# A hybrid mLSTM and delta-rule block: each engine's instruction order made with the framework's timeline model

## The chip, the cores and the metric

The kernel runs on one core of one Trainium2 chip. A core has a matrix engine (TensorE, PE in the profile; its weight loads are listed as PEld), three engines for elementwise work (VectorE or DVE, ScalarE or ACT, GpSimd or POOL) and a sync engine (SP) that here only issues transfers. Each engine works through a list of its own; engines wait for each other and for transfers through semaphores. The metric is device time in microseconds for one execution of the program, lower is better; the time of a kernel is the median of its runs.

## What is computed

One encoder layer over 256 tokens of width 2048, batch 1, in float32, followed by a final RMSNorm. Cut to what matters:

```python
mod = silu(c) @ ada_w + ada_b                       # 2048 -> 6 x 2048
h = rms_norm(x, norm_mix_w) * (1 + scale_m) + shift_m
proj = h @ w_in                                     # 2048 -> about 18500 columns
h_a = bidirectional(mlstm_chunkwise, ...)           # 4 heads, keys of 256, values of 512
y_a = (sigmoid(a_o) * rms_norm(h_a)) @ w_branch_a
qkv = silu(centred_depthwise_conv(b_qkv, gdn_conv_w))
o_b = bidirectional(gated_delta_chunkwise, ...)     # 16 heads of 128
y_b = (rms_norm(o_b) * silu(b_z)) @ w_branch_b
x = x + gate_m * ((g_a * y_a + g_b * y_b) @ w_out)
hf = rms_norm(x, norm_ffn_w) * (1 + scale_f) + shift_f
x = x + gate_f * ((silu(gt) * up) @ w_down)         # gt, up = split(hf @ w_gate_up), 5632 wide
return rms_norm(x, norm_final_w)
```

## The kernel before

**Weights and matmuls.** Every large weight is read once from HBM, in pieces of 1 MB, on SP's queue into one of three buffers called `raw`. For the projections the kernel splits both operands into a high and a low half: ACT copies a piece into a rounded high half `wh` (lines 155 and 180), DVE subtracts it from the piece and gives the low half `wl` (lines 156 and 181), and PE adds three products: high by high, low activation by high weight, high activation by low weight (lines 159 and 161 in `fjob`, lines 198, 199 and 201 in `tjob`). There are three buffers of `wh` and three of `wl`, each for half a piece. `fjob` has the weights as stationary operand and gives features by tokens, 256 columns wide; `tjob` has the activations as stationary operand and gives tokens by features, 512 columns wide, with two accumulators for the two halves of the tokens. Accumulators live in a pool of four PSUM banks (`acc`), the small work of the recurrences in another four (`g`).

**Stages.** The first stage computes the norm, the modulation of the mixer and the first 16 column blocks of the input projection in one loop over the 16 blocks of the width (`first`, line 509; loads `ra` and `raw`, DVE lines 470 and 474). Then come the gates, and the delta rule over the 16 heads in four groups: `gdn_phase1` per head, `gdn_invert` and `gdn_blocks` per group, `gdn_phase2` for each pair of heads (its PE steps are called `p`, `pa`, `pb`, `pc`, `po`, `px`). These are chains of small steps through PE, DVE, ACT and POOL. Between their steps the kernel traces pieces of the rest of the input projection, by counts written out by hand: Python generators (`fills`, `stream`) are advanced by `fill(n)` and `drive(gen, n)`. The same is done with mLSTM and the first branch projection (`y_b`). After that follow the second branch projection (`y_a`), the output projection (`o`, weights `wo`), the second norm (`normed`, `moved`, `low`), gate and up projection (`gt`, `up`), and the down projection (`d`), each group of 512 columns after another.

**Background.** The modulation vectors that are needed later are made on DVE (`ada_part`, line 124): 1 MB of `ada_w` is loaded by SP into a `raw` buffer and multiplied by the row of `silu(c)` with a sum along the way. `pump` and `sums` put such a product in after every second or fourth piece of a projection, or at points written out.

**What sets the order.** The Python code only traces instructions, in one sequence for all engines. When the `with tile.TileContext(...)` block of `kernel` is left, the framework makes from that sequence one list for each engine. It plays the program on a model of the machine: each time an engine of the model can take an instruction, it is given, of those whose inputs and buffers are there in the model, the one traced earliest. The list of an engine is the order in which it was given its instructions in that play, and buffers of a pool (`raw`, `wh`, `wl`, `acc`, `g`) go to whoever comes first in it. So the traced sequence is a priority, and the model's times decide where a later instruction goes ahead of an earlier one. Semaphores are put in afterwards, for the order that came out. On the chip each list is then fixed.

**Pins.** `order(ins)` calls `tc.keep_in_program_order`, which keeps an instruction behind everything traced before it on its engine, whatever the model says. Pinned are nearly all vector and scalar instructions and loads of the first stage, the steps of `gdn_invert` and `gdn_blocks`, the decays of mLSTM, the splits `o_split`, the residual of the last column group, the second norm, and the output. Where `tjob` is called with `early`, the first conversions are pinned as well. All other instructions, nearly all matmuls among them, are free.

## Time and profile before

| what | us |
|---|---|
| median of 3 runs | 2047.38 |
| lowest and highest run | 2047.14 and 2054.85 |
| profiled execution, whole | 2052.6 |
| profiled execution, span from first to last instruction | 2050.5 |
| DVE, busy | 1394.8 |
| ACT, busy | 1047.7 |
| HBM read and written | 467.07 MB and 16.82 MB |

The page of the profile gives, for each engine, the time in which it ran at least one instruction. A matmul's record is longer than its share of the stream of matmuls, since they are pipelined: records overlap. "Idle before" is the time between the records of one engine, and the view of the waits says which engine's instruction or which transfer ended it. A matmul appears with the tile that it writes and the tiles that it reads; the same source line can belong to many jobs, so groups are told apart by the tile's name (`acc_b` is the accumulator of a job `b`, `raw_o` the buffer of a weight piece of a job `o`; `acc_o` stands both for mLSTM's output gate and for the output projection).

### The profile page before, as it was taken

The page shows a single profiled execution, that of the slowest core. Times are in us where ns is not written, and L with a number is a line of the kernel's source. Part 1 is how long each engine was busy: PE and PEld are TensorE (multiplying, and loading weights), DVE is VectorE, ACT ScalarE, POOL GpSimd, SP SyncE. Part 2 cuts the span into 40 slices and gives each one's busy share as a digit, 9 for nine tenths or more (in the row PEclk, how much of TensorE's full clock was granted, in tenths as well). Part 3 has the DMA queues.
Part 4 walks back from the last instruction along what each step waited for, and adds up shares of the span by engine and source line. Part 5 has one row for each costly group of instructions (what it writes and reads, how often), then busy time and mean ns, then how long its engine had stood idle before and what let it go on. Part 6 is the DMA issues. An engine that isn't in the chain of part 4 may idle for free.

```text
span 2050.5 us, 27063 instructions
## 1 busy us (share of the span) xinstructions
PE 1963.4 (96%) x10374; PEld 1711.0 (83%) x10374; DVE 1394.8 (68%) x2059; ACT 1047.7 (51%) x1582; POOL 106.4 (5%) x205
## 2 busy tenths in 40 slices
PE   8999999999999899999999998899999999999998
PEld 6887879988989788889878887678888888888886
DVE  5788776777888588765667777766656665555554
ACT  3147548755774667556443443464444444444443
POOL 0002210110101011101100000000000000000000
PEclk9999999999999999999999999999999999999999
DMA  9986664556667565766986677756766766555553
GB/s 400 420 323 214 194 202 155 179 183 226 235 216 227 180 214 213 236 234 248 368 298 229 218 261 286 279 189 242 259 236 253 254 230 225 197 204 201 202 203 142
DMA packets 78962, 485.64 MB, mean 237 GB/s; under 512 B 10585, under 2 KB 15969, under 8 KB 24433
## 3 DMA queue, kind: packets, MB, share of 16 engines
q1 hardware_dynamic: 63360, 450.95, 60.6%
q0 software_dynamic: 8160, 17.88, 3.8%
q10 hardware_dynamic: 7314, 15.10, 1.9%
q8 instruction: 81, 1.33, 0.3%
q14 instruction: 47, 0.39, 0.1%
HBM read 467.07 MB, written 16.82 MB: 236 GB/s over the span
## 4 chain that ended last, share of the span: by engine, by line
PE 67%; DVE 13%; DMA 11%; ACT 6%; issue 3%; POOL 1%; ACTq 0%; SPq 0%; DVEq 0%; POOLq 0%
PE acc_b L159 4%; PE acc_up L199 4%; PE acc_up L201 4%; PE acc_up L198 4%; PE acc_d L199 4%; PE acc_d L201 4%; PE acc_d L198 4%; PE acc_gt L199 4%; PE acc_gt L201 3%; PE acc_gt L198 3%; DMA ra<-ada 3%; PE acc_b L161 2%; DMA ada<-ada 1%; PE acc_yb L199 1%; PE acc_yb L201 1%
## 5 line engine op out<-in xcount | busy, mean ns | idle before, releaser
L181 DVE TENSOR_TENSOR wl_d<-raw_d,wh_d 128x1024 fp32r<-128x1024 f32 x88 | 107.5, 1225 | 105.3 <-ACT wh_d L180 103.1
L181 DVE TENSOR_TENSOR wl_up<-raw_up,wh_up 128x1024 fp32r<-128x1024 f32 x88 | 107.6, 1225 | 100.0 <-ACT wh_up L180 100.0
L124 DVE SCALAR_TENSOR_TENSOR ada<-ada,crow 128x2048 f32<-128x2048 f32 x64 | 146.4, 2287 | 19.5 <-DMA ada<-ada 19.4
L180 ACT ACTIVATE wh_d<-raw_d 128x1024 fp32r<-128x1024 f32 x88 | 92.9, 1056 | 124.5 <-PE acc_d L199 114.3
L181 DVE TENSOR_TENSOR wl_gt<-raw_gt,wh_gt 128x1024 fp32r<-128x1024 f32 x88 | 107.7, 1224 | 70.1 <-ACT wh_gt L180 68.6
L180 ACT ACTIVATE wh_up<-raw_up 128x1024 fp32r<-128x1024 f32 x88 | 92.9, 1056 | 119.9 <-PE acc_up L199 71.6
L159 PE MATMUL acc_b<-hh,wh_b 128*128 128x256 f32 x576 | 141.4, 288 | 9.3 <-ACT wh_b L155 7.7
L180 ACT ACTIVATE wh_gt<-raw_gt 128x1024 fp32r<-128x1024 f32 x88 | 92.9, 1055 | 108.7 <-PE acc_gt L199 61.3
L159 PE MATMUL acc_b<-hl,wh_b 128*128 128x256 f32 x576 | 138.9, 284 | 0.0
L199 PE MATMUL acc_gt<-wh_gt,hfl 128*128 128x512 f32 x352 | 136.3, 387 | 0.1
L198 PE MATMUL acc_gt<-wh_gt,hfh 128*128 128x512 f32 x352 | 135.2, 384 | 0.0
L199 PE MATMUL acc_up<-wh_up,hfl 128*128 128x512 f32 x352 | 133.6, 379 | 0.0
L198 PE MATMUL acc_up<-wh_up,hfh 128*128 128x512 f32 x352 | 133.5, 379 | 0.0
L198 PE MATMUL acc_d<-wh_d,ffh 128*128 128x512 f32 x344 | 130.8, 380 | 0.0
L199 PE MATMUL acc_d<-wh_d,ffl 128*128 128x512 f32 x344 | 130.7, 380 | 0.0
L159 PEld LDWEIGHTS acc_b<-hh,wh_b 128*128 128x128 f32 x576 | 114.4, 199 | 10.1 <-ACT wh_b L155 8.4
L509 PE MATMUL first<-x,raw 128*128 128x256 f32 x512 | 114.5, 382 | 7.7 <-ACT x L502 7.7
L509 PEld LDWEIGHTS first<-x,raw 128*128 128x128 f32 x512 | 96.2, 190 | 26.0 <-ACT x L502 13.7
L159 PEld LDWEIGHTS acc_b<-hl,wh_b 128*128 128x128 f32 x576 | 114.4, 199 | 0.0
L180 ACT ACTIVATE wh_o<-raw_o 128x1024 fp32r<-128x1024 f32 x64 | 66.2, 1054 | 77.1 <-DMA raw_o<-wo 44.9
L298 DVE SCALAR_TENSOR_TENSOR cv<-pad,pk,cv 128x256 f32<-128x256 f32 x192 | 90.8, 481 | 19.2 <-ACT cv L296 17.1
L156 DVE TENSOR_TENSOR wl_b<-raw_b,wh_b 128x1024 fp32r<-128x1024 f32 x72 | 86.8, 1219 | 24.6 <-ACT wh_b L155 24.2
(369 smaller groups left out, 5031.5 us busy)
## 6 DMA issues: line engine op xcount, KB each, us to landing
ada<-ada SPq DMA_DIRECT2D x64, 1024.0 KB, 4.9
raw_gt<-wgu SPq DMA_DIRECT2D x44, 1024.0 KB, 5.0
raw_up<-wgu SPq DMA_DIRECT2D x44, 1024.0 KB, 5.0
raw_d<-wd SPq DMA_DIRECT2D x44, 1024.0 KB, 4.9
raw_b<-winb SPq DMA_DIRECT2D x36, 1024.0 KB, 5.1
ra<-ada SPq DMA_DIRECT2D x32, 1025.0 KB, 15.7
raw<-win SPq DMA_DIRECT2D x16, 1024.0 KB, 14.5
raw_z<-wint SPq DMA_DIRECT2D x16, 1024.0 KB, 5.1
```

The lines of the kernel that those rows point to most:

```text
L124: V.scalar_tensor_tensor(raw, raw, 1.0, row_c[:, :D], ALU.mult, ALU.mult, accum_out=mod[:, c0 + b : c0 + b + 1])
L156: V.tensor_tensor(wl, raw[:, k0 : k0 + 8], wh.bitcast(F32), ALU.subtract)
L159: PE.matmul(o, wh[:, k], both(x, k0 + k).rearrange("p a b -> p b a"), start=k0 + k + i == 0, stop=False)
L161: PE.matmul(o, wl[:, k], both(hh, k0 + k).rearrange("p a b -> p b a"), start=False, stop=k0 + k == KB - 1)
L180: order(S.activation(wh, raws[u][:, k0 : k0 + 2], AF.Copy), early)
L181: order(V.tensor_tensor(wl, raws[u][:, k0 : k0 + 2], wh.bitcast(F32), ALU.subtract), early)
L198: order(PE.matmul(ps[t], tok(xh, kk, t), turns(wh[:, k]), start=kk == 0, stop=False), early and steps > 1)
L199: PE.matmul(ps[t], tok(xl, kk, t), turns(wh[:, k]), start=False, stop=False)
L201: PE.matmul(ps[t], tok(xh, kk, t), turns(wl[:, k]), start=False, stop=kk == last)
L298: V.scalar_tensor_tensor(cv, pd[:, i : i + T], w[i], cv, ALU.mult, ALU.add)
L509: PE.matmul(first[o], raw[:, o], x[:, b], start=b == 0 and o % 2 == 0, stop=b == KB - 1 and o % 2 == 1)
```

## The change

One argument is given where the context is opened:

```diff
-    with tile.TileContext(nc) as tc:
+    with tile.TileContext(nc, schedule_with_timeline_sim=True) as tc:
         hybrid_block(tc, *args)
```

By default the play that makes the lists runs on the framework's plain simulator, where an engine carries out one instruction at a time for a cost from a table. [...] Nothing else differs: the traced sequence, the pins, the pools and their sizes, and the instructions themselves are those of before. What can differ is the place of each free instruction in its engine's list, which tile gets which buffer of its pool and when, and so the waits that the framework puts in.

## The prediction

> **What bounds the kernel now.** I read the page first, then the windows view cut at the borders of the stages, then the waits of each engine inside a stage.
>
> ```profile
> span 2050.5 us, 27063 instructions
> PE 1963.4 (96%) x10374; PEld 1711.0 (83%) x10374; DVE 1394.8 (68%) x2059; ACT 1047.7 (51%) x1582; POOL 106.4 (5%) x205
> PE 67%; DVE 13%; DMA 11%; ACT 6%; issue 3%; POOL 1%; ACTq 0%; SPq 0%; DVEq 0%; POOLq 0%
> ```
>
> TensorE is the bound by a wide margin: it is busy for 1963.4 of 2050.5 us, and two thirds of the chain that ended last are its instructions. What a new order can win is therefore at most the 87.1 us in which it has no record. Where those lie shows in the windows view (PE, PEld, DVE, ACT, POOL busy with counts, then granted clock, DMA share, GB/s). The stages, by the first and last matmul of each, are: first projection; gates, delta rule and the rest of the input projection; mLSTM with the two branch projections; output projection and second norm; gate/up; down projection.
>
> ```profile
> 0.00:138.00 138.00, 127.65 (x555) 104.31 (x555) 94.08 (x112) 31.59 (x60) 2.41 (x12) 1.00 0.97 399
> 138.00:963.00 825.00, 786.87 (x4948) 709.22 (x4947) 628.25 (x1219) 535.84 (x954) 89.29 (x169) 0.98 0.62 209
> 963.00:1224.00 261.00, 252.03 (x1202) 211.15 (x1201) 179.41 (x223) 115.29 (x148) 14.69 (x24) 0.97 0.74 272
> 1224.00:1357.00 133.00, 113.65 (x487) 92.29 (x486) 97.39 (x125) 59.59 (x91) 0.00 (x0) 0.95 0.70 258
> 1357.00:1808.00 451.00, 450.94 (x2122) 392.64 (x2120) 269.42 (x248) 202.50 (x217) 0.00 (x0) 1.00 0.66 236
> 1808.00:2050.00 242.00, 232.29 (x1071) 201.41 (x1069) 126.27 (x136) 102.91 (x115) 0.00 (x0) 0.99 0.55 191
> ```
>
> Idle time is window less PE busy: 10.4, 38.1, 9.0, 19.4, 0.1 and 9.7 us, 86.7 together. Gate/up has none: 2122 matmuls in 451 us, one every 0.2125 us, at clock 1.00. So only the middle three stages, 66.5 us, can be moved by an order. The first stage is at 0.97 of the DMA engines, and its loads, vector work and conversions are pinned one behind the other by `order`; only its matmuls are free. The end of the last stage is the output, pinned too.
>
> **The change, part by part.** It adds and removes no instruction of the kernel's own: no matmul, conversion or DMA. What it moves is the place of every unpinned instruction on PE, ACT, DVE, SP and POOL, since each list is made by a play of the program through another model. A faithful model can win what an order can win, a wrong one can lose far more than that. So I price by stage.
>
> *Gate/up and down (693 us).* ACT has a conversion ready to start and waits until PE lets a buffer go:
>
> ```profile
> ACT wh_d L180 <- PE acc_d L199: 114.3, 75, 2.0
> ```
>
> 75 waits for 88 conversions mean that supply is ahead of PE almost always. I cost the new order here at 0. The cover is that wait, 114.3/75 = 1.5 us for each conversion, and three buffers of 12 matmuls each, 36 x 0.2125 = 7.7 us. An instruction put ahead of a conversion that takes longer than this would show as idle PE. Below nothing is excluded: there is no idle time to win.
>
> *Gates, delta rule and projections (825 us).* This is where the lists are least pinned. All waits of PE in this stage (us in total, times, longest):
>
> ```profile
> PE acc_b L159 <- ACT wh_b L155: 7.7, 4, 4.0
> PE acc_z L198 <- ACT wh_z L180: 4.8, 3, 2.8
> PE p L687 <- DVE R L659: 4.8, 2, 2.5
> PE vps L553 <- ACT vf L299: 3.5, 5, 1.7
> PE acc_o L201 <- DVE wl_o L181: 3.4, 1, 3.4
> PE acc_mb L201 <- DVE wl_mb L181: 2.4, 3, 1.2
> PE acc_z L201 <- DVE wl_z L181: 1.8, 2, 1.2
> PE acc_v L201 <- DVE wl_v L181: 1.7, 1, 1.7
> PE acc_b L161 <- DVE wl_b L156: 1.6, 1, 1.6
> PE acc_b L159 <- ACT ev_ma L311: 1.6, 1, 1.6
> PE p L696 <- DVE pt L688: 1.5, 1, 1.5
> PE px L770 <- ACT obt L772: 1.0, 1, 1.0
> PE pb L745 <- DVE r L746: 0.8, 1, 0.8
> PE acc_ma L201 <- DVE wl_ma L181: 0.8, 1, 0.8
> PE p L721 <- DVE pt L710: 0.3, 1, 0.3
> ```
>
> Two of the waits of ACT in the same stage:
>
> ```profile
> ACT wh_b L155 <- DMA raw_b<-winb: 15.0, 7, 6.0
> ...
> ACT wh_z L180 <- DMA raw_z<-wint: 11.3, 3, 6.3
> ```
>
> PE's rows sum to 37.7 us in 28 waits, 1.35 us each. Three kinds. (i) The waits for `wh_b` and `wh_z`, 12.5 us: the conversion itself waits for a landing, as these two rows show, so another order on ACT alone gains nothing. (ii) Those for the low halves `wl` (11.7) and `ev_ma` (1.6), 13.3 us: DVE or ACT was at something else, and an order can cure it. (iii) Those of the delta rule's chain (`p`, `vps`, `px`, `pb`), 11.9 us: PE stood at a step of the chain; an order that has a projection matmul in that place cures it if one was ready. The gain lies between 0 and 13.3 + 11.9 = 25.2 us. I take half, 12.6 us, as nothing in the trace shows that more was ready at those moments.
>
> Against it stand the waits that the new order makes itself. The trace of before cannot show them, and the bounds are wide: 0 if every instruction lands where it is wanted, and for one displaced instruction the longest wait above, 4.0 us. The nearest row is the mean, 1.35 us. DVE and ACT are 76% and 65% busy here (628.25 and 535.84 of 825), so a list drawn from another model misplaces something too; I take about as many as vanish, 9 x 1.35 = 12.2 us. What is queued behind such an instruction on DVE is the next `wl`, and behind that SP, since a `raw` buffer comes free only when its `wl` is made:
>
> ```profile
> SPq L177 <- DVE wl_z L181: 78.8, 10, 15.6
> ```
>
> A late `wl` thus delays a load as well, and the load the next conversion. Net for the stage: -12.6 + 12.2 = -0.4 us, with 25.2 us as the end on the gain's side; the other end is the rival on DVE below.
>
> Idle time is not all that a wait costs: clock 0.98 over 825 us is 16.5 us of full-clock work not granted, beside 38.1 us of idle, so each us of new idle may cost up to 1.43 us. I put this in the range, not in the sum. [...]
>
> *mLSTM and branch projections (261 us).*
>
> ```profile
> PE pxa L978 <- DVE hal L983: 3.6, 1, 3.6
> PE psc L922 <- DMA mkq<-kq_d: 3.5, 1, 3.5
> ```
>
> Two waits make 7.1 of the 9.0 us idle. The second is a landing; the first is a step with nothing else ready. Bounds: 7.1 us gained; lost, as much again. I take 0.
>
> *Output projection and second norm (133 us).*
>
> ```profile
> PE acc_o L198 <- ACT wh_o L180: 8.2, 5, 3.5
> PE pxn L1169 <- ACT xn L1162: 7.9, 7, 3.4
> PE acc_o L201 <- DVE wl_o L181: 3.2, 3, 1.8
> ```
>
> ```profile
> ACT wh_o L180 <- DMA raw_o<-wo: 44.9, 10, 8.5
> ```
>
> The norm (7.9) is pinned. The 11.4 us at `acc_o` have a landing behind them: ACT waits 44.9 us for `raw_o`, since loads of `wo` and of `ada` share the three `raw` buffers and the SP list. If the new SP list has the `wo` loads earlier, up to 11.4 us go; if it has more `ada` loads ahead of them, as much comes. I take 0.
>
> *Sum.* -0.4 us against the profiled execution: its span of 2050.5 us is 2052.6 us with what lies around it, 5.2 us above the median of the three runs, 2047.38 us. The same difference on the median gives 2047.0 us.
>
> **The rivals.**
>
> *B, the waits are filled.* If the model has semaphores, queues and transfers about as the chip has them, its play stalls where the chip stalls and puts ready matmuls there. All of (ii) and (iii) go: 2047.4 - 25.2 = 2022 us. With the clock that comes back (0.43 x 25.2 = 11 us) and the 7.1 us of mLSTM it is 2004 us; with half, 2035 us. For it: the waits are short and scattered, and projections are waiting for buffers at nearly all times. Against it: PE is at 96%, and 12.5 us of the waits come from landings.
>
> *C, slower: a modulation product in front of a low half on DVE.* The products of `ada_part` are ready as soon as their load lands, and nobody needs them before the output projection.
>
> ```profile
> L181 DVE TENSOR_TENSOR wl_d<-raw_d,wh_d 128x1024 fp32r<-128x1024 f32 x88 | 107.5, 1225 | 105.3 <-ACT wh_d L180 103.1
> ```
>
> ```profile
> L124 DVE SCALAR_TENSOR_TENSOR ada<-ada,crow 128x2048 f32<-128x2048 f32 x64 | 146.4, 2287 | 19.5 <-DMA ada<-ada 19.4
> ```
>
> ```profile
> 138.00:963.00 825.00, 50.49 (x44) 0.98 0.62 209
> ```
>
> If an engine's list takes what is ready first, a 2.29 us product stands ahead of a 1.2 us `wl`. It decides from the point where the converted lead is below 2.29 + 1.2 = 3.5 us, out of the 7.7 us of three buffers. 44 products lie in the stage (last row: the stage's window, this line alone); if a third meets a low lead, 15 x 2.29 = 34 us: 2081 us. All 44 would give 2148 us, past any range I believe. For it: DVE at 76% and SP behind its `wl`. Against it: the same products stand free in the list of now, and the waits for `wl` are 11.7 us in all.
>
> *D, slower: more table loads and a later chain.* Nothing pins ACT's functions of the delta rule against the sigmoids of the projections.
>
> ```profile
> L299 ACT ACT_TABLE_LOAD x21 | 26.9, 1283 | 0.4
> ```
>
> Twenty more loads are 26 us of ACT; on a chain that PE waits for, nearly all of it shows: 2073 us. [...]
>
> *The change does nothing:* lists that come out the same would give 2047 us; it lies inside the forecast.
>
> **How the numbers follow.** About 0.5% (10 us) is what a measurement of this kernel can tell from no change. A, the forecast, 2037 to 2057 us: 0.32. B, 2004 to 2037 us: 0.29. C, 2057 to 2148 us: 0.26. D, 2057 to 2101 us: 0.13. So A is the likeliest single case, and the time is 2047 us, its own range 2037 to 2057 us. Faster is B, 0.29; same is A, 0.32; slower is C and D, 0.39. The range leaves out the better end of B (0.07) and the worse ends of C and D (0.12): 2018 to 2088 us.
>
> **What would show it.** Gate/up again with 0.1 us idle and one matmul every 0.2125 us: that supply there does not hang on the order. PE idle in the second stage near 38 us, with other pairs in the list: A. Near 13 us: B. New rows of PE waiting for `wl` with L124 ahead on DVE, and SP waiting longer for `wl`: C. Twenty more table loads on ACT, most of them in the second stage: D; as many as now: D is out. I am wrong altogether if gate/up shows idle PE, if the first stage leaves 0.97 of the DMA engines, or if a stage's matmul count per us changes without idle time.

## The result and the profile after

The kernel after takes 2038.43 us (median of 7 runs, 2033.41 to 2042.76), the kernel before beside it 2052.63 us (7 runs, 2047.14 to 2056.65). The ratio is 0.9931 with a 95% interval of 0.9917 to 0.9946: 14.2 us or 0.69% faster. On the earlier median that is 2047.38 x 0.9931 = 2033 us. The profiled execution took 2041.08 us, 11.5 less than the one of before. The page of the kernel after:

```profile
span 2039.0 us, 27090 instructions
...
PE 1955.7 (96%) x10374; PEld 1712.5 (84%) x10374; DVE 1388.3 (68%) x2059; ACT 1035.5 (51%) x1571; POOL 105.8 (5%) x205
```

The matmuls are the same 10374; ACT has 11 instructions fewer, all of them table loads. The windows view of the kernel after (window, its length, then busy time and count of PE, PEld, DVE, ACT and POOL, granted clock, DMA share, GB/s): first the second stage in the borders of before, then the stages in their own borders.

```profile
138.00:963.00 825.00, 792.63 (x5052) 720.50 (x5051) 628.96 (x1214) 527.08 (x940) 88.81 (x169) 0.98 0.65 214
...
138.00:981.00 843.00, 810.63 (x5148) 736.53 (x5147) 638.34 (x1231) 537.41 (x959) 88.81 (x169) 0.98 0.64 213
981.00:1221.00 240.00, 225.66 (x1022) 186.77 (x1021) 167.94 (x219) 102.08 (x134) 14.63 (x24) 0.96 0.76 274
1221.00:1347.00 126.00, 109.65 (x466) 89.29 (x465) 93.27 (x116) 57.09 (x89) 0.00 (x0) 0.93 0.70 258
1347.00:1796.00 449.00, 449.00 (x2121) 393.55 (x2120) 268.37 (x248) 203.68 (x217) 0.00 (x0) 1.00 0.66 237
```

In the same 825 us the kernel after does 104 matmuls more (5052 for 4948). Gate/up again has no idle time. The waits of PE in the second stage of the kernel after (in total, times, longest):

```profile
PE acc_z L201 <- DVE wl_z L181: 7.2, 1, 7.2
PE acc_b L159 <- ACT wh_b L155: 6.5, 6, 1.6
PE vps L553 <- ACT vf L299: 3.3, 2, 3.1
PE p L687 <- DVE R L659: 3.1, 1, 3.1
PE p L721 <- DVE pt L710: 2.9, 3, 2.2
PE px L770 <- DVE on L790: 2.5, 2, 2.0
PE pb L745 <- ACT z L737: 2.0, 2, 1.0
PE px L770 <- ACT obt L772: 1.4, 1, 1.4
...
PE acc_v L201 <- DVE wl_v L181: 0.6, 1, 0.6
```

One new wait of 7.2 us stands at the start of the stage (150.3 to 157.5 us). Beside it the waits for `wl`, 11.7 us before, are down to 0.6 us, and the waits for `wh_z` are gone. In the two stages behind (first fence mLSTM, second fence output projection):

```profile
PE acc_yb L198 <- ACT obh L897: 11.2, 1, 11.2
PE acc_yb L201 <- DVE wl_yb L181: 2.8, 1, 2.8
```

```profile
PE pxn L1169 <- ACT xn L1162: 8.9, 7, 5.3
PE acc_o L198 <- ACT wh_o L180: 7.4, 6, 2.9
```

Since both kernels run the same matmuls, they can be compared at equal work. Each matmul is weighted with the median pace of its form, 1916.6 us in all; the table has the time at which that much PE work is done, and for the other kernels the difference from before at that point (run 8, with another traced sequence, is left out). It is worked out from the traces, one execution of each kernel. Two executions of the kernel before differ by some 4 to 6 us on the mean, and its 31 runs beside runs 5 to 8 spread over 17 us; the entries from 300 to 650 move by 2 to 3 us with the way in which forms are told apart.

```
us of PE work              150     300     450     650     850     950    1200    1900
before                   170.1   333.4   490.4   712.3   924.2  1030.6  1306.9  2023.7
after                     +4.8    -8.3    -9.9   -10.4   -13.4    -3.5   -10.5   -12.3
1 all lists pinned        +4.9    -8.1    -9.8   -12.3   -16.6   -10.0   -24.5   -23.4
2 early lists             +4.9    -7.9    -7.5    -9.8   -12.4    -5.0   -10.4    -9.9
3 late lists              -0.8    +0.3    -0.6    +2.6    +0.9    +5.6    -7.2    -7.1
4 after, last8            +4.8    -8.1    -8.2   -14.0   -16.7    -8.8   -22.7   -12.1
5 PE's list               -0.0    -3.5    -6.7    -6.5    +6.7   +16.3    +4.0    +4.4
6 DVE's and ACT's lists   +4.7    -7.6   -12.0   -13.0   -10.6    -1.0    -6.8    -7.1
7 after, wl free          +7.8    -5.0    -6.8   -12.3   -16.6    -7.7   -21.3   -20.3
9 ACT's list              +9.1    +7.4    +9.6    +2.8   +27.4   +36.5   +26.3   +26.9
10 DVE's list             +7.4    -4.6    -6.2    -5.4    +2.2    +8.5    -1.5    +1.6
11 after, last chain      +4.9    -8.0    -8.1   -10.0   -14.1    +4.3    -6.6    -4.6
12 before, last8          -0.9    -0.2    +0.4    +6.0    +8.1   +11.3    +8.4   +15.8
```

The kernel after is behind at 150 us of work (the new wait), ahead from 300 on, and most at 850. Then it loses 9.9 us, wins 7.0 back by 1200, and keeps what it has. The lead is made in the second stage; runs 2 and 3 below say the same of the time.

**Where a wait went.** ACT's timeline of the kernel before around its longest wait, 4.0 us for `wh_b` at 689 us (start, duration, engine, line, operation, tiles; in brackets the idle time ahead of it and what ended it):

```profile
684.42 1.06 ACT L155 ACTIVATE wh_b<-raw_b 128x1024 fp32r<-128x1024 f32 x1 [6.01 <-DMA raw_b<-winb]
...
686.71 1.69 ACT L667 ACTIVATE X<-cg 32x256 f32<-32x256 f32 x4
688.41 0.55 ACT L717 ACTIVATE UL<-p 32x128 f32<-32x128 f32 x2
...
690.50 1.69 ACT L672 ACTIVATE UL<-cg 32x256 f32<-32x256 f32 x4
692.20 1.06 ACT L155 ACTIVATE wh_b<-raw_b 128x1024 fp32r<-128x1024 f32 x1
```

The first half of a piece is made at 684.42, when it has landed; the second half, which needs no other landing, follows 7.8 us later, with ACT busy nearly all the while at 18 short steps of the delta rule and its convolution that stand ahead of it in the list. PE has run dry by then. The same stretch in the kernel after:

```profile
690.96 2.01 ACT L155 ACTIVATE wh_b<-raw_b 128x1024 fp32r<-128x1024 f32 x2 [2.85 <-DMA raw_b<-winb]
692.87 0.36 ACT L294 ACTIVATE pad<-acc_b 128x256 f32<-128x256 f32 x1
```

Both halves are made one behind the other, and the chain's copies follow. Between 600 and 650 us of work, around this place, the kernel after gains 9.3 us (it is 1.1 us ahead at 600 and 10.4 at 650); the waits of PE in that stretch make 10.2 us before and 3.0 after.

**Where a new wait came from.** The last step of the delta rule, `px`, ends at 980.9 us instead of 963.1, while the projections that stand beside it end earlier (`acc_ma` at 986.7 instead of 1007.7). mLSTM's buffers open only when the delta rule's are closed (the first loads of `o4` go out at 986.4 us, 966.4 before), so PE stands 11.2 us at `acc_yb`, the row above; run 1 below shows how much of this hangs on the late chain. Why the chain is late shows in DVE's timeline of the kernel after, and then in ACT's:

```profile
914.94 2.29 DVE L124 SCALAR_TENSOR_TENSOR ada<-ada,crow 128x2048 f32<-128x2048 f32 x1 [5.41 <-DMA ada<-ada]
917.16 0.08 DVE L124 DVE_READ_ACCUMULATOR ada<-ada,crow 128x1 f32 x1
917.16 1.22 DVE L181 TENSOR_TENSOR wl_o<-raw_o,wh_o 128x1024 fp32r<-128x1024 f32 x1
918.29 0.41 DVE L746 TENSOR_TENSOR r<-vv,pb 128x256 f32<-128x256 f32 x1
```

```profile
922.45 1.06 ACT L180 ACTIVATE wh_o<-raw_o 128x1024 fp32r<-128x1024 f32 x1 [5.74 <-DMA raw_o<-wint]
923.41 0.35 ACT L737 ACTIVATE z<-pc,sm 128x128 f32<-128x128 f32 x1
```

`pb` is done at 911.7 us, but its `r` stands in DVE's list behind a product of the modulation, for whose load DVE waits 5.41 us: 6.6 us late. `pc` is done at 919.5, and its `z` stands on ACT behind a `wh_o` that waits for a landing: 3.9 us late. In the kernel before the same two steps start 0.1 us after `pb` and `pc`, so these two make some 10 of the 17.8 us.

### The profile page after: what moved, and what is told of

Read it like the earlier page. It is cut to its first block, busy times and chain, and to the rows that moved or that the text cites. A ratio compares the mean times of both kernels' runs of the same rounds, so it can differ in the third digit from the quotient of the medians.

```text
span 2039.0 us, 27090 instructions
## 1 busy us (share of the span) xinstructions
PE 1955.7 (96%) x10374; PEld 1712.5 (84%) x10374; DVE 1388.3 (68%) x2059; ACT 1035.5 (51%) x1571; POOL 105.8 (5%) x205
## 4 chain that ended last, share of the span: by engine, by line
PE 74%; DMA 9%; DVE 8%; ACT 6%; issue 2%; POOL 0%; ACTq 0%; SPq 0%; DVEq 0%; POOLq 0%
PE acc_up L198 4%; PE acc_up L201 4%; PE acc_up L199 4%; PE acc_d L201 4%; PE acc_d L198 4%; PE acc_d L199 4%; PE acc_gt L198 4%; PE acc_gt L199 4%; PE acc_gt L201 4%; DMA ra<-ada 2%; PE acc_b L159 2%; PE acc_a L159 2%; PE first L509 2%; DMA raw_b<-winb 2%; PE acc_o L201 2%
## 5 line engine op out<-in xcount | busy, mean ns | idle before, releaser
L509 PEld LDWEIGHTS first<-x,raw 128*128 128x128 f32 x512 | 97.3, 192 | 25.0 <-ACT x L502 11.9
L155 ACT ACTIVATE wh_b<-raw_b 128x1024 fp32r<-128x1024 f32 x72 | 75.3, 1057 | 58.3 <-DMA raw_b<-winb 30.8
## 6 DMA issues: line engine op xcount, KB each, us to landing
ra<-ada SPq DMA_DIRECT2D x32, 1025.0 KB, 15.2
```

The source lines that it names most:

```text
L155: S.activation(wh, raw[:, k0 : k0 + 8], AF.Copy)
L509: PE.matmul(first[o], raw[:, o], x[:, b], start=b == 0 and o % 2 == 0, stop=b == KB - 1 and o % 2 == 1)
```

## The experiments

The lists of an engine can be carried from one model to the other. A helper (its core is shown, the rest left out) schedules the same traced program in a scratch context with the wished model (timeline with the argument of the change, plain without it) and returns the order; a second one then ties each instruction of an engine to the one ahead of it in that order, by an edge that needs no semaphore:

```python
for n in ordered:
    i = traced[n]
    if type(i).__name__ == "BassTilePoolBoundary" or not kept(n):
        continue
    if i.engine in last:
        tc.add_manual_dep(
            i, last[i.engine].name,
            mybir.DependencyInfo(mybir.DependencyClass.NoSync, mybir.DependencyReason.DATA), reason="pinned",
        )
    last[i.engine] = i
```

What is not tied stays free in the plain play. `CUT` is the place in the traced sequence where mLSTM begins, behind the delta rule.

### 1 to 3: which part of the program

```diff
-        hybrid_block(tc, *args)
+        hybrid_block(tc, *args); _pin(tc, timeline, lambda n: n < CUT[0]); _pin(tc, timeline, lambda n: n >= CUT[0]) # 1
+        hybrid_block(tc, *args); _pin(tc, timeline, lambda n: n < CUT[0]); _pin(tc, plain, lambda n: n >= CUT[0])    # 2
+        hybrid_block(tc, *args); _pin(tc, plain, lambda n: n < CUT[0]); _pin(tc, timeline, lambda n: n >= CUT[0])    # 3
```

> The lists of the timeline play are pinned, engine by engine, in a plain play (in two parts, cut where mLSTM's pools are opened), so this should be the changed kernel again. Every theory: 14 us under the kernel before, ratio 0.993; if it is the lists and nothing else that the change acts through, the interval holds 0.993. A ratio of 1.000 would say that the pins don't carry the lists over.

> Timeline lists for what is traced up to the end of the delta rule, plain lists for the rest. Theory 1 (PE gets some 13 us ahead in the delta stage, then loses about 10 because the recurrence ends late and the first branch projection waits for it, then gains about 9 later): 3 to 5 us under the kernel before, 0.998. Theory 2 (the gain is made in the delta stage and stays): 12 to 14 us under it, 0.9935. Theory 3 (the gain is all in the output projection): no difference, 1.000.

> Plain lists up to the end of the delta rule, timeline lists for the rest. Theory 1: 8 to 10 us under the kernel before, 0.9955. Theory 2: no difference, 1.000. Theory 3: 12 to 14 us under it, 0.9935.

Measured, against 2049.78 us for before on that chip: all lists 2033.3 us (0.9918, interval 0.989 to 0.9946); early lists 2038.49 us (0.9942, 0.992 to 0.9964); late lists 2047.56 us (0.9989, 0.9973 to 1.0005). The lists alone, in a plain play, carry the whole gain. Of it, 0.58% comes with the lists up to the end of the delta rule, and nothing that can be measured with those behind.

By their traces, the lists of run 1 on PE, DVE and ACT are those of the kernel after but for one place, the border of the two parts: 199 matmuls, 26 steps on DVE and 36 on ACT stand elsewhere, from 943 us on. There the steps of the last pair of heads come earlier, and `px` ends at 960.4 us instead of 980.9. So run 1 is also the test of the late chain, and most of the wait of PE stays:

```profile
PE acc_yb L198 <- ACT obh L897: 7.5, 1, 7.5
```

The loads that `obh` needs go out at 963.4 us and have landed by 970.3, but `obh` stands in ACT's list behind a `wh_yb` that waits for its own piece:

```profile
986.57 1.06 ACT L180 ACTIVATE wh_yb<-raw_yb 128x1024 fp32r<-128x1024 f32 x1 [4.70 <-DMA raw_yb<-wbb]
...
990.65 2.00 ACT L897 ACTIVATE obh<-o 128x1024 fp32r<-128x1024 f32 x2 [0.63 <-DMA raw_yb<-wbb]
```

In run 2, with `px` at 966.4 us, there is no wait for `obh` at all, and 6.0 us for a `wh_ma` in its place. The time of neither run can be told from that of after: the intervals overlap.

### 4: a shorter last chain in the kernel after

```diff
-    last = (0, 1, 2, 1, 2, 2, 1, 1, 3, 0)
+    last = (0, 1, 1, 1, 1, 1, 1, 1, 1, 0)
```

> The changed kernel with fewer projection pieces traced between the steps of the last two pairs of heads (8 for each pair instead of 13), so that they are left as cover behind the end of the recurrence. Theory 1: the 11 us wait of the first branch projection for obh goes, PE idle in that place under 3 us: 2028 us, 0.988. Rival (the wait only changes place, since the loads behind it or the mLSTM steps are late as well): 2038 us, 0.993.

A miss of both: 2043.7 us, ratio to before 0.9972 (0.9955 to 0.9989), slower than after. The wait stayed:

```profile
PE acc_yb L198 <- ACT obh L897: 11.4, 1, 11.4
```

The two holds of `r` and `z` are gone here, and the chain ends at 974.3 us; but the projections beside it end earlier as well, `acc_ma` at 981.0 instead of 986.7. Fewer pieces traced between the steps did not keep the play from running the later ones ahead. What the run loses, it loses behind that: its lead is 22.7 us at 1200 us of work and 12.1 at 1900.

### 5, 6, 9 and 10: which engine's list

All four tie only the named engines, up to `CUT`, and leave everything else free in the plain play:

```diff
-    if type(i).__name__ == "BassTilePoolBoundary" or not kept(n):
+    if type(i).__name__ == "BassTilePoolBoundary" or not kept(n) or i.engine.name not in ('PE',):                   # 5
+    if type(i).__name__ == "BassTilePoolBoundary" or not kept(n) or i.engine.name not in ('DVE', 'Activation'):     # 6
+    if type(i).__name__ == "BassTilePoolBoundary" or not kept(n) or i.engine.name not in ('Activation',):           # 9
+    if type(i).__name__ == "BassTilePoolBoundary" or not kept(n) or i.engine.name not in ('DVE',):                  # 10
```

> Only PE's list up to the end of the delta rule is the timeline model's; ACT, DVE, POOL and SP are free in the plain play, and so is all that comes later. Theory P (the gain is in the order of the matmuls: high products of the next half ahead of the low products of this one): most of the 11.9 us that all five lists of this part gave together, that is 8 to 12 us below the kernel before, waits of PE for wl in the second stage 0 to 2 us instead of 11.7, and as many table loads as before, 68, give or take 4. Theory V (the gain is in DVE's and ACT's lists, which have 11 table loads fewer and put the steps of the chains earlier): within 3 us of the kernel before. Rival M (the lists only fit each other): slower than before by more than 5 us.

> Only DVE's and ACT's lists up to the end of the delta rule are the timeline model's; PE, POOL and SP are free in the plain play. Theory P: within 3 us of the kernel before, waits of PE for wl near 10 us. Theory V: 8 to 12 us below before, with 57 table loads. Rival M: slower by more than 5 us. If P and V each hold in part, this and the run with PE's list alone give some 6 us each.

> Only ACT's list up to the end of the delta rule is the timeline model's; all other engines are free in the plain play. PE's list alone was slower by 0.49% though it, too, left only 56 table loads, so the table loads carry nothing. Theory V1 (DVE's order carries what DVE's and ACT's lists gave together, 10.6 us by 850 us of PE work): this one is within 3 us of the kernel before at that point and at the end. Theory V2 (ACT's order, with the steps of the chains and the copies wh that it brings forward, carries it): 7 to 11 us ahead at 850 us of PE work, and 3 to 8 us below before at the end.

> Only DVE's list up to the end of the delta rule is the timeline model's. Theory V1: 7 to 11 us ahead of the kernel before at 850 us of PE work, and 3 to 8 us below it at the end. Theory V2: within 3 us at both. Theory M2 (the two lists need each other): neither this run nor that with ACT's list alone is more than 4 us ahead at 850 us.

| lists of the timeline model | ratio to before | interval | table loads |
|---|---|---|---|
| all five (run 2) | 0.9942 | 0.992 to 0.9964 | 57 |
| DVE and ACT (run 6) | 0.9979 | 0.9962 to 0.9996 | 57 |
| DVE (run 10) | 1.0034 | 1.002 to 1.0049 | 62 |
| PE (run 5) | 1.0049 | 1.0032 to 1.0065 | 56 |
| ACT (run 9) | 1.0122 | 1.0102 to 1.0142 | 57 |

Neither PE's, DVE's nor ACT's list gives the gain; each alone makes the kernel slower, ACT's by 1.22%. POOL's and SP's alone were not tried. DVE's and ACT's together are 12 to 13 us ahead from 450 to 650 us of work and then lose most of it; only with PE's, POOL's and SP's as well does more of it stay (the intervals of runs 2 and 6 just touch). So theories P and V both fall, and so do V1 and V2; what holds is M2, and M in the form that the lists fit each other. Fewer table loads do not make the kernel faster by themselves: 56 in the slower run 5, 68 in before. The two costliest waits of PE with ACT's list alone, second stage:

```profile
PE p L687 <- DVE R L659: 8.9, 3, 5.9
PE acc_z L198 <- ACT wh_z L180: 6.9, 1, 6.9
```

The other engines are again put in order by the plain model, which presumably believes ACT to be elsewhere in its list than the chip has it; no run shows the play itself.

### 7: the new wait of 7.2 us taken away

In `halves` the low halves of the first job `z` from the fifth on are no longer pinned behind the gate steps:

```diff
-            order(V.tensor_tensor(wl, raws[u][:, k0 : k0 + 2], wh.bitcast(F32), ALU.subtract), early)
+            order(V.tensor_tensor(wl, raws[u][:, k0 : k0 + 2], wh.bitcast(F32), ALU.subtract), early and (steps > 1 or u < 2))
```

> The kernel after, with the low halves of the first job z from its fifth half on no longer pinned behind the gate steps. Theory: the one wait of PE for wl_z of 7.2 us, and the 4.8 us by which the kernel after is behind at 150 us of PE work, are the pin's doing, since DVE's list has the convolution's steps between the gate steps ahead of it. Then this kernel is 5 to 7 us below after: some 18 to 21 us below before (ratio 0.990 to 0.991), and the wait is under 1 us. Rival: the gate steps come later by what the low halves take, their chain starts the delta rule later, and the time is that of after within 3 us (ratio 0.993 to 0.9945).

2038.72 us, ratio 0.9951 (0.9931 to 0.9971): the time of after, so the rival holds in the time, though by another way than it said. The wait moved to the next step:

```profile
PE acc_z L198 <- ACT wh_z L180: 10.2, 1, 10.2
```

Run 7 and the kernel after are both on the gain's side at 300 us of work. The 3 us by which run 7 is further behind at 150 are still there at 300 and 450 and gone at 650. As a wait stands at this place in both, neither says what the kernel would gain without it.

### 8: the mechanism by hand, in the plain play

In the jobs of the input projection, the low products of one half of a piece are traced behind the high products of the next half, so that DVE has longer to make `wl`:

```diff
-            for kk, k, t in kt:
-                PE.matmul(ps[t], tok(xh, kk, t), turns(wl[:, k]), start=False, stop=kk == last)
+            lows = ([] if not n else lows) + [(wl, kt)]
+            for wl, (kk, k, t) in [(w, q) for w, kq in (lows if n == len(todo) - 1 else lows[:-1] if xh is hh else lows) for q in kq]: PE.matmul(ps[t], tok(xh, kk, t), turns(wl[:, k]), start=False, stop=kk == last)
+            lows = lows[-1:] if xh is hh else []
```

and the same in `fjob`.

> The kernel before, plain model, with one change of the traced sequence in the jobs of the input projection: the low products of a half stand behind the high products of the next half of the same job. Theory P: this alone gives DVE one half's high products (8 x 0.2125 = 1.7 us or more) for each wl, so the waits for wl in the second stage fall from 11.7 us to under 3 us, and the time is 6 to 10 us below before (ratio 0.995 to 0.997). Theory V: as before within 3 us, because other waits take their place.

2047.92 us, ratio 0.9981 (0.9965 to 0.9998). Of the 6 to 10 us some 4 came (0.4 to 7 by the interval); waits for `wl` of 8.8 us stayed, and `wh_z` and `px` took the place of the others:

```profile
PE acc_z L198 <- ACT wh_z L180: 5.4, 2, 5.1
PE acc_v L201 <- DVE wl_v L181: 4.2, 3, 2.2
...
PE px L771 <- ACT obt L773: 3.8, 2, 3.6
```

### 11: the last chain at high priority in the kernel after

```diff
-                next(pairs[p], None)
+                with tc.high_priority() if g == 3 else ExitStack(): next(pairs[p], None)
```

> The kernel after, with the steps of the last group of heads (phase 2 of group 3) traced at high priority, so that the play takes them ahead of any projection that is ready. Theory: the idle 11.2 us of PE before the first y_b comes from the last chain's late end (px at 980.9 us instead of 963.1), so with the chain first it ends 8 to 15 us earlier, the idle time shrinks to under 3 us, and the time is 6 to 10 us below after (ratio to before 0.988 to 0.990). Rival: the chain is bound by its own steps and not by its place in the lists; it ends within 3 us of where it did, and the time is that of after (ratio 0.993 to 0.995).

2039.48 us, ratio 0.9949 (0.993 to 0.9967): the rival. `px` ended at 981.1 us, and PE stood as long:

```profile
PE acc_yb L198 <- ACT obh L897: 10.4, 2, 9.5
PE acc_yb L199 <- DVE obl L898: 3.5, 1, 3.5
```

`r` still stands behind the same product of the modulation (DVE waits 5.44 us for its load) and starts at 917.2 us. Priority moves a step ahead of what is ready in the play; presumably the play has the load in time where the chip has it late, which no run shows. Runs 4 and 11 did not shorten the wait; runs 1 and 2 did, without a gain that can be told from noise.

### 12: the model or one list among many

The edit of run 4 in the kernel before.

> The kernel before, plain model, with the edit that the kernel after had in the fourth run: for the last group of heads one piece of projection between two steps, eight in all in place of twelve. It asks whether the gain belongs to the model or to one list among many. Theory S (the timeline model's lists are better as such): the edit costs here about what it cost there, 0.4%, so the ratio to before is 1.000 to 1.006, and the kernel after with this edit (0.9972) stays 0.3 to 0.9% below it. Theory L (any small edit draws another list, good or bad by several us whatever the model): the ratio may be 0.993 to 0.997, and the two with the edit are within 0.2% of each other.

2064.39 us, ratio 1.0073 (1.0051 to 1.0095). The edit costs 0.73% with the plain model and 0.41% with the timeline model (0.9972 over 0.9931), and with it the two are 1.0% apart. An edit draws another list; this one cost 15 us and 8 us. But all programs whose lists come wholly from the timeline model (after, runs 1, 4, 7 and 11) lie at 0.9918 to 0.9972, and the plain ones (before, runs 8 and 12) at 0.9981 to 1.0073. So the gain is the model's, as far as five programs and three can show it (the intervals of runs 4 and 8, the nearest of the two kinds, overlap), and its size depends on the list that is drawn. Run 1 is the best here, with an interval that overlaps that of after; no version beat after beyond doubt.

## Why the prediction was right and wrong

The range, 2018 to 2088 us, held the time, which says little: it is 70 us wide and takes in a part of every rival. The forecast, no change at 2047 us with 2037 to 2057 us as its own range, did not hold it: the time on its scale is 2033 us, the half-way case that rival B gave as 2035 us.

**The bound, and the stages that cannot move: right.** Gate/up has 449.00 of 449.00 us busy and one matmul every 449/2121 = 0.2117 us; from 1200 us of work to the end, in which gate/up and down lie, the table moves by 1.8 us. The first stage keeps 0.97 of the DMA engines.

**The step that failed: "I take about as many as vanish", the net of -0.4 us in the second stage.** It was -13.4 us at 850 us of PE work. Two terms were mis-sized. Kind (ii), 13.3 us, fell to the 0.6 us and one new wait of 7.2 us, of which no run shows what it costs at the end. And kind (i), 12.5 us at `wh_b` and `wh_z`, was put down to landings and priced at nothing; it fell to 6.5 us. ACT's timeline shows that its longest, 4.0 us, was order-made: the landing was the first half's, the wait the second half's. The waits view shows the releaser of the matmul, not what stood ahead of that releaser in its own list; the timeline of the releasing engine would have shown it before. So new waits did come, but for less than vanished: the view of the second stage after has 32.2 us in 25 waits, that of before 37.7 in 28. Kind (iii) even grew: the chain's rows in the fence above make 15.2 us, and 16.8 with those under 0.7 us, for 11.9 before. So B, which had (ii) and (iii) go, has, at one half, the size about right, and one of its two sources wrong.

**Clock beside idle time: seen, and small here.** From 138 us to 850 us of work PE is idle for 37.9 us before and 30.4 after:

```profile
138.00:924.20 786.20, 748.26 (x4709) 674.19 (x4708) 607.53 (x1190) 512.43 (x914) 89.29 (x169) 0.98 0.62 208
```

```profile
138.00:910.80 772.80, 742.37 (x4681) 672.96 (x4680) 601.29 (x1176) 499.83 (x885) 88.81 (x169) 0.98 0.65 213
```

So 7.5 of the 13.4 us are idle time and 5.9 us are shorter busy time; the clock's records make it 15.4 us of full-clock work lost before and 13.7 after, 1.7 us of these, or 0.23 us for each us of idle time, where the prediction allowed up to 0.43 (run 9, below, has 1.1). The rest, some 4 us, stays open: records of matmuls overlap (in gate/up of after a record of 128x512 takes 0.379 us, and the next matmul starts 0.216 us after it did, both medians), so that busy time is not a measure of pace. In run 9 the price is plain: at the same work 52.3 us idle (14.3 more) and 30.7 us lost to the clock (15.4 more) for 27.4 us:

```profile
138.00:951.60 813.60, 761.35 (x4688) 683.39 (x4688) 606.01 (x1178) 498.27 (x885) 89.81 (x169) 0.96 0.61 202
```

**Rival C** had the right instruction and the wrong victim: a modulation product does stand ahead of something on DVE, but of the chain's `r`, and with its load not yet landed. **Rival D** is out in its first half: 57 table loads for 68, not twenty more. No run shows the term that takes its range up to 2101 us: each of these loads took 1.283 us, before and after, and twenty more of them give its 2073 us. Its second half came, the later chain, 17.8 us late at the end. A wait of 11.2 us follows it in the mLSTM stage, forecast at 0 within 7.1 us (run 1 has 7.5 of them without the late chain); the table loses 9.9 us there, less than the wait, as the projections had been run ahead. **The output projection**, forecast at 0 within 11.4 us, won some 2.5 us (8.0 us ahead at 1150 us of work, 10.5 at 1250), less than two executions of one kernel differ by.

What the runs do not say is which property of the timeline model makes its set of lists fit the chip better. That the gain needs several lists at once (runs 5, 6, 9, 10) speaks for its times as a whole and against one habit such as low products behind high ones (run 8), but this is argued, not shown.

## What to carry to other kernels

A list is good or bad with the other engines' lists: here all lists together gained 0.69% (after) and 0.82% (run 1), and the order of one engine alone, with the others left to the plain play, lost 0.34 to 1.22%. So try a model's lists for all engines together before those of one. When a wait is priced by what ended it, look in the releasing engine's timeline at what stood ahead of the releaser, since "behind a landing" can be "behind 18 short steps". Work that waits for a load and stands in a list ahead of a chain's step holds that step up as well, here by 6.6 and 3.9 us, and high priority in the traced sequence did not cure it (run 11). And ask whether something else holds the same instruction before a late chain is repaired: run 1 ended the chain 20 us earlier and kept 7.5 of the 11.2 us.

## What the runs showed of the hardware

In the traces of before and after, TensorE's granted clock was 1.0 or 0.5, and within the span it stayed at 0.5 for 3.41, 6.83, 10.24 or 13.65 us. The windows view of the kernel before around one stretch of 3.41 us, in steps of that length:

```profile
211.87:215.28 3.41, 3.41 (x22) 3.10 (x21) 3.41 (x9) 2.71 (x5) 0.00 (x0) 1.00 0.85 303
215.28:218.69 3.41, 1.71 (x12) 1.23 (x11) 3.41 (x6) 2.48 (x4) 1.29 (x3) 1.00 0.49 183
218.69:222.10 3.41, 3.41 (x11) 2.87 (x11) 2.21 (x10) 2.24 (x6) 0.00 (x0) 0.50 0.85 72
222.10:225.50 3.40, 3.40 (x18) 2.98 (x17) 2.00 (x2) 1.06 (x1) 0.00 (x0) 1.00 0.93 361
```

In the second row PE has no record for 1.7 us, and in the third the clock is 0.50, which is 1.7 us of full-clock work not granted. The two traces have 26 stretches of half clock. Two close the span, and one, at 1113.0 us of before, has no idle PE in the 3.41 us ahead of it; the 3.41 us ahead of each of the other 23 have 1.47 us or more of idle PE. Of the gaps of PE of 2.6 us and more, all 14 had half clock within 3.41 us of their end or lay in it; of those of 1.5 to 2.6 us 8 of 20, of those of 1.0 to 1.5 us 1 of 11, and of those of 0.5 to 1.0 us none of 21. So in these two traces 22 of the 34 waits of 1.5 us or more stood beside half clock, at 1.7 us of work for each 3.41 us of it.
